# FFN second product of a two-layer decoder trunk: row tiles in written order in other PSUM banks, the next group's weight sums asked for between them

## The chip, the cores and the metric

One core of a Trainium2 chip runs the whole program. The metric is the device time of one execution in microseconds, the median of several runs. All times below are microseconds (us) unless marked ns. The engines are named as in the profile: PE (TensorE, matmuls), DVE (VectorE), ACT (ScalarE), POOL, and SP, whose queue starts nearly all transfers.

## The reference

Two layers of a decoder trunk for 512 positions of width 1024, in float32. Each layer is a mixer (attention, retention, short convolution, gates, output projection) and then the part that the change touches, a gated MLP with a causal depthwise convolution:

```python
h = rmsnorm(x, norm_ffn_g[l])
gu = jnp.einsum('bsd,df->bsf', h, w_ffn_in[l])
g_ff, u_ff = gu[..., :D_FF], gu[..., D_FF:]          # D_FF = 2816
g_ff = causal_dwconv(g_ff, ffn_conv_w[l], ffn_conv_b[l])
x = x + jnp.einsum('bsf,fd->bsd', jax.nn.silu(g_ff) * u_ff, w_ffn_out[l])
```

## The kernel before, in words

Everything is held transposed: channels on the 128 partitions, 512 positions in the free dimension. x is 8 tiles of 128x512. To keep float32 precision each operand is split into a high and a low part (`split`, `split_w`: ACT casts the high part, DVE subtracts for the low part), and `mm3` issues three matmuls for each product: high x high, high x low, low x high. So each weight tile goes: one transfer on SP's queue into a `raw` buffer (4 of them, shared by all weights), a cast on ACT, a subtraction on DVE, into `hi` and `lo` buffers (3 each for the wide ones).

The FFN (`ffn`) handles the 22 channel tiles f of width 128 in three groups, `GROUPS = (5, 9, 8)`. For each f of a group the first product and the convolution give one tile `act`; then the second product adds the group's contribution to x.

- Group 0 (f = 0 to 4) uses `plain(f)`: two full products `pg` and `pu` of 24 matmuls with 512 columns. In between, `halves(k)` prepares the operands `X` of the other form (tiles xn, xt, X).
- Groups 1 and 2 (f = 5 to 13 and 14 to 21) use `seven(f)`: seven half-width products of 12 matmuls with 256 columns each, made from sums of the weights. DVE forms the sums s31 and s24 from the transfers raw_f0 and raw_f1 (the second half of s31 needs both), ACT and DVE split them into h31/l31 and h24/l24. The products land in two PSUM tiles, `pa` and `pb`. `pa` is overwritten several times; of the fifth product `pa` is added into the tile u by DVE (line 865), and only after that the seventh product may overwrite `pa`. Then come the convolution (ACT line 309, DVE lines 310 and 311, tile c), a Silu, the product u times c (DVE line 874), and the split into `act`.
- `rows(grp, f0, act, d)` is the second product for one row tile d of x: 3 matmuls of 512 columns for each f of the group into the PSUM tile `p2` (15, 27 or 24 matmuls), then DVE adds it to x[d] (line 888). For a group of more than 8, its weights come in two pieces.

PSUM has two pools of four banks, `main` and `aux`. pa, pb, pg, pu and p2 all use `main`.

Which instruction comes when on each engine is not written by hand: a list scheduler with its own estimates of time orders them at build time; each engine then runs its queue strictly in that order. `tc.high_priority()` lifts instructions (weights, their splits and sums), and `tc.keep_in_program_order` ties an instruction to the written order on its engine: it isn't put ahead of what is written before it, though what is written later may still be put ahead of it.

Names in the rows: buffer numbers and the layer's digit are left out, so p210L is p2 of group 1, row 0 (p200L: group 0, row 0; p223L: group 2, row 3), pa13L is pa of f = 13, s3114L is s31 of f = 14, h315L is h31 of f = 5, act13L is act of f = 13. hi_faL, hi_fbL, hi_w2L are the split weights.

Of the kernel before, what the change touches and what calls it, by code (L numbers as in the profile page):

```python
# [24 lines left out]
KT = D // P  # L25
# [3 lines left out]
FT = DFF // P  # L29

GROUPS = (5, 9, 8)
HALF = S // 2
BUCKETS = 32
MAX_DIST = 128
# [19 lines left out]
def trunk(ctx, tc, xT, wr, wh, wt, wda, wret, wsc, wo, wf, w2, par, lamp, relb, onehot, mask, rope, gtab, out):  # L54
# [32 lines left out]
    def run(steps):  # L87
        for _ in steps:
            pass
# [29 lines left out]
    def main(name):  # L119
        return pm.tile([P, S], F32, tag="main", name=name)  # L120

    def aux(name):
        return pa.tile([P, S], F32, tag="aux", name=name)
# [30 lines left out]
    def weights(src, name):  # L154
        return split_w(load_w(src, name), name)

    def mm3(o, a, b, start, stop, more=False):

        T.matmul(o, a[0], b[0], start=start, stop=False, skip_group_check=more)  # L159
        T.matmul(o, a[0], b[1], start=False, stop=False, skip_group_check=more)  # L160
        T.matmul(o, a[1], b[0], start=False, stop=stop, skip_group_check=more)  # L161

    def split(src, hi, lo, g=None):

# [602 lines left out]
    def ffn(l, fp):  # L767
# [4 lines left out]
        L = f"L{l}"  # L772
# [54 lines left out]
            V.tensor_tensor(u, u, c, ALU.mult)  # L827
            return split2(u, pairN(f"act{f}{L}"))

        def seven(f):  # L830
            upper, lower = [load_w(wf[l, f, :, b * D : (b + 1) * D], f"f{b}{L}{f}") for b in range(2)]
            a21, a11, a22, a12 = upper[:, :S], upper[:, S:], lower[:, :S], lower[:, S:]
            with tc.high_priority():
                w11 = split_w(a11, f"fa{L}{f}")
                s31 = fp.tile([P, 2, S], F32, tag="sum", name=f"s31{f}{L}", bufs=2)
                V.tensor_tensor(s31[:, 0], a21, a11, ALU.add)
                V.tensor_tensor(s31[:, 1], a21, a22, ALU.add)
                h31, l31 = slotX(f"h31{f}{L}"), slotX(f"l31{f}{L}")
                split(s31, h31, l31)
                s24 = fp.tile([P, 2, S], F32, tag="sum", name=f"s24{f}{L}", bufs=2)  # L840
                V.tensor_tensor(s24[:, 0], s31[:, 1], a11, ALU.add)
                V.tensor_tensor(s24[:, 1], s24[:, 0], a12, ALU.add)
                h24, l24 = slotX(f"h24{f}{L}"), slotX(f"l24{f}{L}")
                split(s24, h24, l24)
                w2212 = split_w(lower, f"fb{L}{f}")
            w22, w12 = [tuple(t[:, b * S : (b + 1) * S] for t in w2212) for b in range(2)]

            def product(o, w, b, start, stop):
# [27 lines left out]

        def rows(grp, f0, act, d):

            ps = main(f"p2{grp}{d}{L}")
            width = len(act)  # L880
            edge = min(width, KT // 2) if width > KT else 0
            for a, b in ((0, edge), (edge, width)):
                if a < b:
                    w = weights(w2[l, d, :, (f0 + a) * P : (f0 + b) * P], f"w2{L}{grp}{d}{a}")
                    for n in range(a, b):
                        sl = slice((n - a) * P, (n - a + 1) * P)
                        mm3(ps, (w[0][:, sl], w[1][:, sl]), act[n], n == 0, n == width - 1)
            V.scalar_tensor_tensor(x[d], ps, -1.0 if grp else 1.0, x[d], ALU.mult, ALU.add)
            if l == DEPTH - 1 and grp == len(GROUPS) - 1:
                nc.sync.dma_start(out[:, d], x[d])  # L890

        f0 = 0
        todo = list(range(KT // 2))
        for grp, width in enumerate(GROUPS):
            act = []
            for f in range(f0, f0 + width):
                act.append(seven(f) if grp else plain(f))
                if f == 1:
                    late.close()
                if grp == 0 and f and todo:  # L900
                    halves(todo.pop(0))
            for d in range(KT):
                rows(grp, f0, act, d)
            f0 += width

    for l in range(DEPTH):
# [107 lines left out]
```

## Time and profile before

| | us |
|---|---|
| median of 3 runs | 1522.0 |
| lowest and highest run | 1521.76, 1523.62 |
| the profiled execution's own time | 1522.98 |
| its span, first to last instruction | 1521.2 |
| PE busy | 1512.6 (99%) |
| DVE busy | 1105.0 (73%) |
| ACT busy | 734.0 (48%) |
| transfers, mean | 97 GB/s |

The profile is of one execution. Its own time is 1.8 above its span. The granted TensorE clock is 1.00 over the whole span. Matmuls overlap in the records: a matmul of 512 columns is shown with 390 ns while the next starts 227 ns after it, so time that PE lost is read from the distance of the starts, not from the column of idle time alone.

### The profile page before, as it was taken

How to read it: one execution, taken by the hardware profiler on the slowest of the kernel's cores; microseconds unless marked ns; L12 is line 12 of the kernel's file. 1: busy time of each engine (PE TensorE's matmuls, PEld its weight loads, DVE VectorE, ACT ScalarE, POOL GpSimd, SP SyncE). 2: the span in 40 equal slices, each digit the busy share in tenths (PEclk: the TensorE clock that was granted, in tenths of full speed). 3: DMA queues.
4: the chain of work that ended last, by engine and by line, in shares of the span. 5: the costliest groups of instructions: out<-in, count | busy, mean ns of one | idle time of the engine just before them, and what ended most of it. 6: DMA issues, size and time to landing. Idle time of an engine off the chain costs nothing.

```text
span 1521.2 us, 22083 instructions
## 1 busy us (share of the span) xinstructions
PE 1512.6 (99%) x8510; PEld 1338.7 (88%) x8510; DVE 1105.0 (73%) x2074; ACT 734.0 (48%) x1304; POOL 13.0 (1%) x26
## 2 busy tenths in 40 slices
PE   9999999999999999999999999999999999999998
PEld 7899988888888999899789999888888889988996
DVE  8588787554688995796656887875545889947963
ACT  4555665333454564464425565643333546634641
POOL 1000000000000000000100000000000000000000
PEclk9999999999999999999999999999999999999999
DMA  6322222232323322522322222222322233324322
GB/s 212 115 73 81 86 84 90 76 104 83 106 74 107 118 92 72 169 84 84 131 77 94 74 91 87 83 84 83 106 88 86 79 113 112 97 84 139 111 59 81
DMA packets 51146, 147.24 MB, mean 97 GB/s; under 512 B 5624, under 2 KB 6023, under 8 KB 51041
## 3 DMA queue, kind: packets, MB, share of 16 engines
q1 hardware_dynamic: 50224, 143.38, 28.7%
q0 software_dynamic: 816, 2.46, 0.6%
q8 instruction: 67, 1.10, 0.3%
q14 instruction: 39, 0.31, 0.1%
HBM read 143.70 MB, written 2.11 MB: 96 GB/s over the span
## 4 chain that ended last, share of the span: by engine, by line
PE 97%; DVE 1%; DMA 1%; issue 0%; ACT 0%; SPq 0%; ACTq 0%; DVEq 0%
PE pnrvgL L161 1%; PE pnrvgL L159 1%; PE pnrvgL L160 1%; PE pnrqkL L160 1%; PE pnrqkL L161 1%; PE pnrqkL L159 1%; PE pnh2L L161 1%; PE pnh2L L159 1%; PE pnh3L L160 1%; PE pnh3L L161 1%; PE pnh1L L161 1%; PE pnh2L L160 1%; PE pnh3L L159 1%; PE pnh1L L160 1%; PE pnh1L L159 1%; PE pnh0L L160 1%
## 5 line engine op out<-in xcount | busy, mean ns | idle before, releaser
L150 ACT CAST hi_tL<-raw_tL 128x1024 fp32r<-128x1024 f32 x60 | 62.9, 1049 | 115.3 <-issue 14.7
L150 ACT CAST hi_w2L<-raw_w2L 128x640 fp32r<-128x640 f32 (+2 forms) x64 | 49.1, 782 | 94.0 <-PE p210L L160 11.2
L151 DVE TENSOR_TENSOR lo_tL<-raw_tL,hi_tL 128x1024 fp32r<-128x1024 f32 x60 | 73.4, 1223 | 15.9 <-ACT hi_tL L150 15.5
L151 DVE TENSOR_TENSOR lo_w2L<-raw_w2L,hi_w2L 128x640 fp32r<-128x640 f32 (+2 forms) x64 | 55.8, 888 | 29.5 <-ACT hi_w2L L150 29.5
L150 ACT CAST hi_fbL<-raw_f1L 128x1024 fp32r<-128x1024 f32 x34 | 35.7, 1051 | 32.3 <-PE pa5L L160 5.7
L150 ACT CAST hi_oL<-raw_oL 128x1024 fp32r<-128x1024 f32 x16 | 16.9, 1054 | 58.1 <-issue 18.7
L151 DVE TENSOR_TENSOR lo_fbL<-raw_f1L,hi_fbL 128x1024 fp32r<-128x1024 f32 x34 | 41.6, 1222 | 1.5 <-ACT hi_fbL L150 1.4
L150 ACT CAST hi_faL<-raw_f0L 128x512 fp32r<-128x512 f32 x34 | 21.1, 620 | 30.7 <-DMA raw_f0L<-in_wf 12.8
L151 DVE TENSOR_TENSOR lo_faL<-raw_f0L,hi_faL 128x512 fp32r<-128x512 f32 x34 | 23.4, 689 | 4.0 <-ACT hi_faL L150 3.9
L150 ACT CAST hi_nrvgL<-raw_nrvgL 128x1024 fp32r<-128x1024 f32 x8 | 8.4, 1051 | 29.7 <-PE pnrvgL L161 13.5
L150 ACT CAST hi_fuL<-raw_fuL 128x1024 fp32r<-128x1024 f32 x10 | 10.5, 1054 | 22.9 <-issue 17.1
L151 DVE TENSOR_TENSOR lo_oL<-raw_oL,hi_oL 128x1024 fp32r<-128x1024 f32 x16 | 19.6, 1224 | 2.8 <-ACT hi_oL L150 2.8
L151 DVE TENSOR_TENSOR lo_nrvgL<-raw_nrvgL,hi_nrvgL 128x1024 fp32r<-128x1024 f32 x8 | 9.8, 1226 | 12.4 <-ACT hi_nrvgL L150 12.4
L150 ACT CAST hi_fgL<-raw_fgL 128x1024 fp32r<-128x1024 f32 x10 | 10.5, 1050 | 14.8 <-issue 13.0
L151 DVE TENSOR_TENSOR lo_nh0L<-raw_nh0L,hi_nh0L 128x768 fp32r<-128x768 f32 x8 | 7.7, 958 | 13.1 <-ACT hi_nh0L L150 13.1
L150 ACT CAST hi_bdL<-raw_bdL 128x512 fp32r<-128x512 f32 x16 | 9.9, 618 | 12.6 <-issue 4.2
L150 ACT CAST hi_nrqkL<-raw_nrqkL 128x1024 fp32r<-128x1024 f32 (+1 forms) x9 | 8.4, 948 | 13.9 <-issue 13.9
L151 DVE TENSOR_TENSOR lo_fuL<-raw_fuL,hi_fuL 128x1024 fp32r<-128x1024 f32 x10 | 12.2, 1222 | 2.9 <-ACT hi_fuL L150 2.9
L150 ACT CAST hi_nh0L<-raw_nh0L 128x768 fp32r<-128x768 f32 x8 | 6.7, 838 | 15.2 <-PE pnh0L L161 7.8
L151 DVE TENSOR_TENSOR lo_nrqkL<-raw_nrqkL,hi_nrqkL 128x1024 fp32r<-128x1024 f32 (+1 forms) x9 | 9.9, 1109 | 5.2 <-ACT hi_nrqkL L150 5.2
L151 DVE TENSOR_TENSOR lo_fgL<-raw_fgL,hi_fgL 128x1024 fp32r<-128x1024 f32 x10 | 12.2, 1222 | 0.8 <-ACT hi_fgL L150 0.8
L150 ACT CAST hi_nh3L<-raw_nh3L 128x768 fp32r<-128x768 f32 x8 | 6.7, 838 | 11.5 <-PE ptg16L L160 5.3
(8471 smaller groups left out, 5969.6 us busy)
## 6 DMA issues: line engine op xcount, KB each, us to landing
raw_tL<-in_wt SPq DMA_DIRECT2D x60, 512.0 KB, 3.3
raw_f0L<-in_wf SPq DMA_DIRECT2D x34, 512.0 KB, 3.8
raw_f1L<-in_wf SPq DMA_DIRECT2D x34, 512.0 KB, 3.7
raw_w2L<-in_w SPq DMA_DIRECT2D x32, 320.0 KB, 2.9
raw_oL<-in_wo SPq DMA_DIRECT2D x16, 512.0 KB, 3.4
raw_w2L<-in_w SPq DMA_DIRECT2D x16, 512.0 KB, 3.5
raw_fgL<-in_wf SPq DMA_DIRECT2D x10, 512.0 KB, 4.0
raw_fuL<-in_wf SPq DMA_DIRECT2D x10, 512.0 KB, 4.0
```

Source lines behind the costliest of these rows:

```text
L150: A.copy(h, raw)
L151: V.tensor_tensor(w, raw, h.bitcast(F32), ALU.subtract)
L159: T.matmul(o, a[0], b[0], start=start, stop=False, skip_group_check=more)
L160: T.matmul(o, a[0], b[1], start=False, stop=False, skip_group_check=more)
L161: T.matmul(o, a[1], b[0], start=False, stop=stop, skip_group_check=more)
```

## The change

`mm3` gets an option that ties its matmuls to the written order, and `rows` uses it. `rows` takes its PSUM tile from `aux` instead of `main`. It becomes a generator that stops ahead of the last f of its group, and the loop first runs 2, 1 and 1 row tiles (`AHEAD`) of groups 0, 1 and 2 up to that point; then all row tiles are run to their ends one after the other. `seven` is cut in two: `sums(f)` (transfers, sums, splits of the sums) and the products; inside a group the sums of f + 1 are written ahead of the products of f, and the sums of the first two f of the next group are written behind row tiles 2 and 5 (`EARLY`) of this one. The split of the lower weights moves from the sums to the products.

```diff
+AHEAD = (2, 1, 1)
+EARLY = (2, 5)
@@
-    def mm3(o, a, b, start, stop, more=False):
-
-        T.matmul(o, a[0], b[0], start=start, stop=False, skip_group_check=more)
-        T.matmul(o, a[0], b[1], start=False, stop=False, skip_group_check=more)
-        T.matmul(o, a[1], b[0], start=False, stop=stop, skip_group_check=more)
+    def mm3(o, a, b, start, stop, more=False, queue=False):
+
+
+        for i, (p, q) in enumerate(((0, 0), (0, 1), (1, 0))):
+            t = T.matmul(o, a[p], b[q], start=start and i == 0, stop=stop and i == 2, skip_group_check=more)
+            if queue:
+                tc.keep_in_program_order(t)
@@
-        def seven(f):
+        def sums(f):
+
             upper, lower = [load_w(wf[l, f, :, b * D : (b + 1) * D], f"f{b}{L}{f}") for b in range(2)]
@@
                 split(s24, h24, l24)
-                w2212 = split_w(lower, f"fb{L}{f}")
+            return lower, w11, h31, l31, h24, l24
+
+        def seven(f, lower, w11, h31, l31, h24, l24):
+            w2212 = split_w(lower, f"fb{L}{f}")
@@
-            ps = main(f"p2{grp}{d}{L}")
+            ps = aux(f"p2{grp}{d}{L}")
@@
                     for n in range(a, b):
+                        if n == width - 1:
+                            yield
                         sl = slice((n - a) * P, (n - a + 1) * P)
-                        mm3(ps, (w[0][:, sl], w[1][:, sl]), act[n], n == 0, n == width - 1)
+                        mm3(ps, (w[0][:, sl], w[1][:, sl]), act[n], n == 0, n == width - 1, queue=True)
@@
+        made = {}
         for grp, width in enumerate(GROUPS):
             act = []
             for f in range(f0, f0 + width):
-                act.append(seven(f) if grp else plain(f))
+                if grp:
+                    for n in (f, f + 1):
+                        if n < f0 + width and n not in made:
+                            made[n] = sums(n)
+                    act.append(seven(f, *made[f]))
+                else:
+                    act.append(plain(f))
@@
+
+            begun = [rows(grp, f0, act, d) for d in range(KT)]
+            for d in range(AHEAD[grp]):
+                next(begun[d])
             for d in range(KT):
-                rows(grp, f0, act, d)
+                run(begun[d])
+                if d in EARLY and grp + 1 < len(GROUPS):
+                    n = f0 + width + EARLY.index(d)
+                    made[n] = sums(n)
```

The number of instructions is the same on every engine; only their order changes, and the lines are numbered some lines later. Three places of the new order follow; layer 1 has the same order at each of them.

The first is DVE at the end of group 0, from the first use of the last product (u4 = pu4 times the norm) to the low part of act4. X2 and X3 are operands that `halves` prepares, s315 is the weight sum of f = 5. Before:

```order
L167 TENSOR_TENSOR X2L_3927<-xt2L_4309,X2L_3927 128x1024
L826 TENSOR_TENSOR u4L_4388<-pu4L_4351,rBfL_4030 128x512
L796 SCALAR_TENSOR_TENSOR xn3L_4394<-x_85,par_110,rBfL_4030 128x512
L796 SCALAR_TENSOR_TENSOR xn7L_4396<-x_89,par_110,rBfL_4030 128x512
L151 TENSOR_TENSOR lo_w2L_4459<-raw_w2L_4456,hi_w2L_4458 128x640
L827 TENSOR_TENSOR u4L_4388<-u4L_4388,c4L_4359 128x512
L800 TENSOR_TENSOR xt3L_4398<-xn3L_4394 128x256
L167 TENSOR_TENSOR X3L_3928<-xn3L_4394,X3L_3928 128x256
L802 TENSOR_TENSOR xt3L_4398<-xn7L_4396,xn3L_4394 128x256
L167 TENSOR_TENSOR X3L_3928<-xn7L_4396,X3L_3928 128x512
L801 SCALAR_TENSOR_TENSOR xt3L_4398<-xt3L_4398,xn7L_4396 128x256
L167 TENSOR_TENSOR act4L_4391<-u4L_4388,act4L_4391 128x512
```

With the change, from u4 to the last row ahead of act4:

```order
L832 TENSOR_TENSOR u4L_4388<-pu4L_4351,rBfL_4030 128x512
L173 TENSOR_TENSOR X2L_3927<-xt2L_4309,X2L_3927 128x1024
L802 SCALAR_TENSOR_TENSOR xn3L_4394<-x_85,par_110,rBfL_4030 128x512
L802 SCALAR_TENSOR_TENSOR xn7L_4396<-x_89,par_110,rBfL_4030 128x512
L155 TENSOR_TENSOR lo_w2L_4459<-raw_w2L_4456,hi_w2L_4458 128x640
L833 TENSOR_TENSOR u4L_4388<-u4L_4388,c4L_4359 128x512
L806 TENSOR_TENSOR xt3L_4398<-xn3L_4394 128x256
L843 TENSOR_TENSOR s315L_4486<-raw_f0L_4478 128x512
L844 TENSOR_TENSOR s315L_4486<-raw_f0L_4478,raw_f1L_4480 128x512
L173 TENSOR_TENSOR X3L_3928<-xn3L_4394,X3L_3928 128x256
L808 TENSOR_TENSOR xt3L_4398<-xn7L_4396,xn3L_4394 128x256
L173 TENSOR_TENSOR X3L_3928<-xn7L_4396,X3L_3928 128x512
```

After these come, as before, the last small xt3 and then act4. Three instructions, the wide split X2 and the two halves of s315, now stand between u4 and act4. On PE, between the last matmul of pu4 and the first matmul that needs the low part of act4, there stand 25 matmuls of 512 columns (24 of row tiles 0 and 1, one of act4's high part) and 14 of 256 columns (pa5 and the start of pb5); before, there were 36 of row tiles 0, 1 and 2 and three of act4's high part.

The second place is PE at the end of group 1: the last matmuls of pa13's fifth product, the seventh product (its weights are hi_fb, lo_fb), and the first row tile. Before:

```order
L161 MATMUL pa13L_5643<-X3L_3928,l3113L_5629 128x256
L159 MATMUL p210L_5745<-act11L_5486,hi_w2L_5766 128x512
L160 MATMUL p210L_5745<-act11L_5486,hi_w2L_5766 128x512
L161 MATMUL p210L_5745<-act11L_5486,lo_w2L_5767 128x512
L159 MATMUL p210L_5745<-act12L_5614,hi_w2L_5766 128x512
L159 MATMUL p211L_5786<-act5L_4718,hi_w2L_5789 128x512
L160 MATMUL p211L_5786<-act5L_4718,hi_w2L_5789 128x512
```

16 more matmuls of p210 and p211 follow before the seventh product begins, 22 in all. With the change:

```order
L165 MATMUL pa13L_5643<-X3L_3928,h3113L_5522 128x256 x2
L165 MATMUL pa13L_5643<-X3L_3928,l3113L_5523 128x256
L165 MATMUL pa13L_5643<-X0L_3925,hi_fbL_5639 128x256 x2
L165 MATMUL pa13L_5643<-X0L_3925,lo_fbL_5640 128x256
L165 MATMUL pa13L_5643<-X1L_3926,hi_fbL_5639 128x256 x2
L165 MATMUL pa13L_5643<-X1L_3926,lo_fbL_5640 128x256
L165 MATMUL pa13L_5643<-X2L_3927,hi_fbL_5639 128x256 x2
L165 MATMUL pa13L_5643<-X2L_3927,lo_fbL_5640 128x256
L165 MATMUL pa13L_5643<-X3L_3928,hi_fbL_5639 128x256 x2
L165 MATMUL pa13L_5643<-X3L_3928,lo_fbL_5640 128x256
L165 MATMUL p210L_5745<-act5L_4740,hi_w2L_5748 128x512 x2
L165 MATMUL p210L_5745<-act5L_4740,lo_w2L_5749 128x512
```

The seventh product now follows the fifth at once, and all 27 matmuls of p210 stand behind it, then p211 and so on. pa21 at the end of group 2 is the same: 24 matmuls of pa21 in a row (before, 12 of pb21, 3 of p220 and 9 of p221 stood between the two products), then p220 to p227, each whole.

The third place is DVE at the same time: from pb13's addition to the low part of u13's product. s3114 and s2414 are the weight sums of f = 14. Before:

```order
L867 TENSOR_TENSOR pad_116<-pad_116,pb13L_5644 128x512
L865 TENSOR_TENSOR u13L_5645<-u13L_5645,pa13L_5643 128x256
L310 SCALAR_TENSOR_TENSOR c13L_5736<-pad_116,par_110,c13L_5736 128x512
L311 SCALAR_TENSOR_TENSOR c13L_5736<-pad_116,par_110,c13L_5736 128x512
L151 TENSOR_TENSOR lo_w2L_5872<-raw_w2L_5869,hi_w2L_5871 128x512
L151 TENSOR_TENSOR lo_w2L_5849<-raw_w2L_5846,hi_w2L_5848 128x640
L874 TENSOR_TENSOR u13L_5645<-u13L_5645,c13L_5736 128x512
L167 TENSOR_TENSOR act13L_5742<-u13L_5645,act13L_5742 128x512
```

With the change:

```order
L877 TENSOR_TENSOR pad_116<-pad_116,pb13L_5644 128x512
L844 TENSOR_TENSOR s3114L_5876<-raw_f0L_5868,raw_f1L_5870 128x512
L875 TENSOR_TENSOR u13L_5645<-u13L_5645,pa13L_5643 128x256
L848 TENSOR_TENSOR s2414L_5883<-s3114L_5876,raw_f0L_5868 128x512
L316 SCALAR_TENSOR_TENSOR c13L_5736<-pad_116,par_110,c13L_5736 128x512
L849 TENSOR_TENSOR s2414L_5883<-s2414L_5883,raw_f1L_5870 128x512
L173 TENSOR_TENSOR l3114L_5880<-s3114L_5876,h3114L_5879 128x1024
L317 SCALAR_TENSOR_TENSOR c13L_5736<-pad_116,par_110,c13L_5736 128x512
L155 TENSOR_TENSOR lo_w2L_5849<-raw_w2L_5846,hi_w2L_5848 128x640
L173 TENSOR_TENSOR l2414L_5887<-s2414L_5883,h2414L_5886 128x1024
L884 TENSOR_TENSOR u13L_5645<-u13L_5645,c13L_5736 128x512
L155 TENSOR_TENSOR lo_w2L_5831<-raw_w2L_5828,hi_w2L_5830 128x512
```

act13's low part is the next row. The second half of s3114, which reads the transfer raw_f1 of f = 14, stands ahead of the addition of pa13, and five instructions on the sums of f = 14 stand between pb13 and u13's product. On SP, raw_f0 and raw_f1 of f = 14 stand behind the weights of row tiles 0 to 2; with four raw buffers, raw_f1 takes the one of row tile 1's second piece of weights, which is free once DVE has split that piece (lo_w2L_5808, five rows above the first row shown, behind the first half of s3114 and both taps of c12). The cast ahead of that split takes a `hi` buffer that PE frees near the end of pa12's seventh product; from there to pa13's seventh product PE has the last matmul of pa12, 1 and 24 of pb13 and 24 of pa13, all of 256 columns.

## Rows read from the trace of the kernel before

**Rows 1.** The profile's first part: engine, busy us (share of the span) and instructions.

```profile
PE 1512.6 (99%) x8510; PEld 1338.7 (88%) x8510; DVE 1105.0 (73%) x2074; ACT 734.0 (48%) x1304; POOL 13.0 (1%) x26
```

**Rows 2.** Who waited for whom on PE: line of the waiting matmul, what it waited for, total us, times, longest us. The idle time is counted from the modelled end of the matmul before.

```profile
PE pa5L L159 <- ACT pad L858: 1.6, 2, 1.0
...
PE p224L L159 <- ACT hi_w2L L150: 0.4, 2, 0.2
```

**Rows 3.** PE in order of time, two steady stretches (start us, duration us, engine, line, operation, tiles, shape): 512 columns, then 256 columns.

```profile
469.16 0.39 PE L159 MATMUL p200L<-act0L,hi_w2L 128*128 128x512 f32 x1
469.38 0.39 PE L160 MATMUL p200L<-act0L,hi_w2L 128*128 128x512 f32 x1
...
500.82 0.28 PE L160 MATMUL pa6L<-X3L,hi_faL 128*128 128x256 f32 x1
500.94 0.28 PE L161 MATMUL pa6L<-X3L,lo_faL 128*128 128x256 f32 x1
```

**Rows 4.** PE and ACT in order of time around pa5's second product (h245), layer 0 and layer 1 (in brackets the idle time before, and what ended it).

```profile
501.34 0.36 ACT L858 COPY pad<-pa5L 128x256 f32<-128x256 f32 x1
...
501.76 0.39 PE L159 MATMUL pa5L<-X0L,h245L 128*128 128x256 f32 x1 [0.54 <-ACT pad L858]
...
501.98 0.28 PE L160 MATMUL pa5L<-X0L,h245L 128*128 128x256 f32 x1
...
1254.74 0.28 PE L161 MATMUL pa6L<-X3L,lo_faL 128*128 128x256 f32 x1
1256.05 0.39 PE L159 MATMUL pa5L<-X0L,h245L 128*128 128x256 f32 x1 [1.03 <-ACT pad L858]
1256.27 0.28 PE L160 MATMUL pa5L<-X0L,h245L 128*128 128x256 f32 x1
```

**Rows 5.** PE in order of time where row tiles 3 to 5 of group 2 begin, first and last row of layer 0 and of layer 1; then ACT at the same place of layer 0.

```profile
734.07 0.39 PE L161 MATMUL p222L<-act21L,lo_w2L 128*128 128x512 f32 x1
...
736.70 0.40 PE L160 MATMUL p225L<-act14L,hi_w2L 128*128 128x512 f32 x1
...
1488.35 0.39 PE L161 MATMUL p222L<-act21L,lo_w2L 128*128 128x512 f32 x1
...
1490.98 0.39 PE L160 MATMUL p225L<-act14L,hi_w2L 128*128 128x512 f32 x1
...
733.37 2.94 ACT L150 CAST hi_w2L<-raw_w2L 128x1024 fp32r<-128x1024 f32 x3 [4.75 <-PE p220L L160]
```

**Rows 6.** PE in order of time where row tiles 3 to 5 of group 0 begin, first and last row of layer 0 and of layer 1.

```profile
479.36 0.40 PE L159 MATMUL p203L<-act0L,hi_w2L 128*128 128x512 f32 x1
...
480.84 0.40 PE L160 MATMUL p205L<-act0L,hi_w2L 128*128 128x512 f32 x1
...
1233.15 0.39 PE L159 MATMUL p203L<-act0L,hi_w2L 128*128 128x512 f32 x1
...
1234.63 0.40 PE L160 MATMUL p205L<-act0L,hi_w2L 128*128 128x512 f32 x1
```

**Rows 7.** DVE in order of time, layer 0: u4 and the low part of act4 at the end of group 0; then pairs of rows that show what one instruction of a kind takes from start to start (a tap of the convolution, a wide split, half of a weight sum).

```profile
469.36 0.69 DVE L826 TENSOR_TENSOR u4L<-pu4L,rBfL 128x512 f32<-128x512 f32 x1 [0.73 <-PE pu4L L161]
...
474.56 0.69 DVE L167 TENSOR_TENSOR act4L<-u4L,act4L 128x512 fp32r<-128x512 f32 x1
...
456.67 0.75 DVE L311 SCALAR_TENSOR_TENSOR c3L<-pad,par,c3L 128x512 f32<-128x512 f32 x1
457.33 1.22 DVE L167 TENSOR_TENSOR X1L<-xt1L,X1L 128x1024 fp32r<-128x1024 f32 x1
...
498.24 1.23 DVE L151 TENSOR_TENSOR lo_fbL<-raw_f1L,hi_fbL 128x1024 fp32r<-128x1024 f32 x1
499.37 1.23 DVE L167 TENSOR_TENSOR l316L<-s316L,h316L 128x1024 fp32r<-128x1024 f32 x1
...
503.44 0.70 DVE L836 TENSOR_TENSOR s317L<-raw_f0L 128x512 f32<-128x512 f32 x1
504.04 0.70 DVE L837 TENSOR_TENSOR s317L<-raw_f0L,raw_f1L 128x512 f32<-128x512 f32 x1
```

**Rows 8.** The turn of pa's fifth product at f = 21, layer 0: its last matmul on PE, and the addition on DVE that waits for it.

```profile
719.24 0.28 PE L161 MATMUL pa21L<-X3L,l3121L 128*128 128x256 f32 x1
...
719.56 0.42 DVE L865 TENSOR_TENSOR u21L<-u21L,pa21L 128x256 f32<-128x256 f32 x1 [4.83 <-PE pa21L L161]
```

**Rows 9.** The profile's list of transfers: count, KB each, median us from issue to landing.

```profile
raw_f1L<-in_wf SPq DMA_DIRECT2D x34, 512.0 KB, 3.7
```

**Rows 10.** ACT and DVE in order of time at the end of group 1, layer 0: the cast of the second piece of a row tile's weights, which waits for pa12, and its split; pa13's addition with the row behind it; u13's product and the low part of act13.

```profile
585.47 0.73 ACT L150 CAST hi_w2L<-raw_w2L 128x640 fp32r<-128x640 f32 x1 [1.98 <-PE pa12L L160]
...
586.23 0.83 DVE L151 TENSOR_TENSOR lo_w2L<-raw_w2L,hi_w2L 128x640 fp32r<-128x640 f32 x1 [2.54 <-ACT hi_w2L L150]
...
591.11 0.42 DVE L865 TENSOR_TENSOR u13L<-u13L,pa13L 128x256 f32<-128x256 f32 x1 [0.75 <-PE pa13L L161]
591.45 0.74 DVE L310 SCALAR_TENSOR_TENSOR c13L<-pad,par,c13L 128x512 f32<-128x512 f32 x1
...
598.94 0.68 DVE L874 TENSOR_TENSOR u13L<-u13L,c13L 128x512 f32<-128x512 f32 x1
600.31 0.69 DVE L167 TENSOR_TENSOR act13L<-u13L,act13L 128x512 fp32r<-128x512 f32 x1 [0.69 <-ACT act13L L166]
```

**Rows 11.** The chain of waits around the first sums of group 1, layer 1: a transfer beside others (start us, us from issue to landing).

```profile
1235.82 5.73 DMA raw_f0L<-in_wf
```

## The prediction

> **What bounds the kernel now.** I read the share of busy time first. PE is busy for 1512.6 of the span of 1521.2 us, DVE for 73%, ACT for 48% [rows 1]. The kernel is bound by PE, and the change neither adds nor removes an instruction; so it can only give back time in which PE stands still, or add some. Next come the waits of PE [rows 2]: they name pa5, which waits for ACT, and the row tiles of group 2, which wait for casts of weights. As the ends of matmuls are modelled, I take the lost time from the starts. In a steady stretch a matmul of 512 columns starts 0.227 us after the one before (469.16 to 469.38) and one of 256 columns 0.12 after it (500.82 to 500.94) [rows 3]; what is longer is lost. Measured so, the FFN loses time at three places in each layer:
>
> - Row tiles 3 to 5 of group 2. From 734.07 to 736.70 there are six steps: 2.63 - 6 x 0.227 = 1.27, and in layer 1 from 1488.35 to 1490.98 the same [rows 5]. Tiles 0 to 2 wait for act21 together, end together, and free three weight buffers at once; the three casts of tiles 3 to 5 take 2.94 in a row, while PE has only two matmuls for each.
> - Row tiles 3 to 5 of group 0, the same in small: 1.48 - 5 x 0.227 = 0.35 in each layer [rows 6].
> - pa5's second product. In layer 0 its first matmuls are at 501.76 and 501.98, the last before them at 500.94 [rows 3, 4]: 1.04 - 2 x 0.12 = 0.80. In layer 1 it is 1.53 - 0.24 = 1.29. ACT's copy of pa5 is late there, behind casts of late weights.
>
> Together 2 x (1.27 + 0.35) + 0.80 + 1.29 = 5.3 us. That is all the change can win in the FFN. A measurement of this kernel can tell a change of 0.2%, 3.0 us, from none.
>
> **What the change removes.** With each row tile run whole, a tile's weights come free 12 to 27 matmuls apart, at least 2.7 us, and a wide cast takes about 1 (2.94 for three) [rows 5]: the two bursts go, -3.2 in all. The first sums of group 1 are asked for some row tiles earlier, so pa5's first product and its copy lie between the row tiles, and the wait of 0.80 and 1.29 goes, -2.1. Putting p2 in other banks gives nothing by itself: what pa5 waits for is a copy out of its own bank [rows 4], not a row tile's.
>
> **What it adds.** The filling matmuls that stood between dependent products are now tied behind them. I go through the FFN's dependent places, for one layer.
>
> (1) act4, end of group 0. On DVE the low part of act4 ends at 475.25, 5.89 after u4 starts [rows 7]. The new order puts a wide split (1.13, from 498.24 to 499.37) and two halves of a sum (0.60 each, 503.44 to 504.04) in between [rows 7]: 8.22. PE starts the row tiles 0.20 before u4 (469.16, 469.36) [rows 3, 7] and has 25 matmuls of 512 columns and 14 of 256 until it needs that part: 25 x 0.227 + 14 x 0.12 = 7.35, so it is there at 7.15. From the end of a releaser to PE's start take 0.06 (501.34 + 0.36 to 501.76) [rows 4]. Wait: 8.22 + 0.06 - 7.15 = 1.13. The first matmul after a wait also costs some 0.10 more (501.76 to 501.98 is 0.22, not 0.12) [rows 4]; this and the wait for h315 just before overlap, so I take **1.2**. Bounds: 0.7 if DVE gets one half of the sum done earlier, 1.5.
>
> (2) pa21, end of group 2. The seventh product now stands right behind the fifth, with DVE's addition between. The addition starts 0.32 after the last matmul's start (719.24, 719.56) and takes 0.42 [rows 8], then 0.06: 0.80 - 0.12 = 0.68, and 0.10 for the slow first matmul: **0.78**. Nothing covers it. Bounds: 0.6 to 0.9.
>
> (3) pa13, end of group 1: the same 0.78 at least, but DVE's queue now holds the second half of s3114 ahead of the addition, and that waits for the transfer raw_f1 of f = 14. Its buffer is freed by the split of row tile 1's second piece, that by a cast which starts when pa12's seventh product lets go of a buffer. Call the cast's start 0. PE's matmul that releases it began 0.32 earlier [rows 8], and with it and 50 more of 256 columns PE is ready for the seventh product at 51 x 0.12 - 0.32 = 5.80. The cast takes 0.73, the split 0.83 and can start at 0.76 [rows 10]; but the first half of s3114 and the two taps of c12 (0.60 + 2 x 0.66, 456.67 to 457.33) [rows 7] stand ahead of it, and no row tells how much of them is left. I take a third, 0.6: the split ends at 2.19, the transfer lands 3.7 later [rows 9] at 5.89, the half sum (0.60) and the addition (0.42) end near 6.95, PE starts at 7.03. Wait 1.23, with the slow start **1.3**. Bounds: 0.78 if the taps are done, 2.6 if none is.
>
> (4) act13, same place. From the addition's start DVE has, in its new order, 0.34 (591.11 to 591.45), two halves of s2414 (2 x 0.60), two taps (2 x 0.66), two wide splits (2 x 1.13) and a split of weights (0.74): 5.86; from u13's product to the end of act13's low part before were 2.06 (598.94 to 601.00) [rows 7, 10]: 7.92, with 0.06 7.98. PE starts the seventh product at 0.48, loses 0.10, has 12 x 0.12 and 25 x 0.227: 7.70. Wait 0.28, with a slow start **0.4**. Bounds: 0 to 0.8. For act21 no sums stand in the way; 2.06 and two taps are well under the 21 x 0.227 = 4.8 of row tile 0.
>
> Sum for a layer 1.2 + 0.78 + 1.3 + 0.4 = 3.7, for both 7.4. Against 5.3 that is +2.1; the transfers being moved earlier on SP's queue cost nothing else, as SP waits for buffers and not for issue, and 16 engines' transfers average 97 GB/s. The profiled execution's span becomes 1523.3 and its own time 1525.0; this execution was 1.0 above the median of 1522.0, so the median becomes **1524.0 us**. Own range by the bounds: 2 x (0.7 + 0.6 + 0.78 + 0) = 4.2 to 2 x (1.5 + 0.9 + 2.6 + 0.8) = 11.6, so 1520.9 to 1528.3, the upper bounds together being unlikely.
>
> A rule that speaks for the change: the Trainium skill, "Perfetto Trace Analysis", section Optimizing Tensor Performance, says that independent groups of matmuls should rotate through different PSUM banks, so that emptying one overlaps the next. By that rule alone, taking p2 out of pa's banks would shorten every handover. By the rows it does nothing here, since the waits are inside one bank (pa) or on weights; where it would lead is rival C.
>
> **Rivals.**
>
> A. It evens out. pa13's transfer is early, (3) falls to 0.78 and (4) to nothing, (1) to 0.9: 2 x 2.5 = 5.0 against 5.3, 1521.7 us. For it: DVE idles before some of these rows (2.54 before the split) [rows 10], so the taps may be done.
>
> B. Slower beyond 0.2%. The transfers of the next group's sums now run among those of the row tiles' weights, and DVE's queue holds instructions that wait for them ahead of what PE needs. Beside others a raw_f0 took 5.73 [rows 11], not 3.7. If raw_f1 of f = 14 takes that, (3) grows by 2.0, in two layers by 4.0: 1528.0 us. It decides as soon as the transfer lands 0.5 later than I take it (2 x 0.5 more makes +3.1). Against it: at that point SP has just waited for a buffer, so little should be under way.
>
> C. Faster. The waits of 5.3 go and none comes, because ACT and DVE are free enough to feed row tiles one by one and the handovers overlap: 1516.7 us. Against it: (2) has no cover at all in the new order, on PE or elsewhere.
>
> That the change doesn't do what it says is ruled out by the new order; but "begun ahead" does nothing at groups 1 and 2, where row tile 0 stands behind all products.
>
> **How the numbers follow.** My forecast 0.55, of which a tenth lies above +3.0; A 0.17, B 0.22, C 0.06. Faster by over 0.2%: 0.06; within: 0.50 + 0.17 = 0.67; slower: 0.22 + 0.05 = 0.27. The range for 8 in 10 leaves out C and the worst of B: from 1521.0, the forecast's lower bound, to 1527.2.
>
> **What would show it right or wrong.** Right: the steps at row tiles 3 to 5 are steady, pa5's second product doesn't wait, and PE loses time instead ahead of p200 (on act4), between the two last products of pa13 and of pa21 (on DVE's line 875), and near the end of p210 (on act13). Wrong: pa21 without a gap; a gap at pa13 over 2 us, released behind a transfer; or new gaps at the first products of a group (pa5, pa14), which I cost at nothing because their weights are asked for several row tiles ahead.

## The result, and the profile after

The changed kernel takes 1525.1 us (median) against 1522.1 for the kernel before beside it: ratio 1.0018, 95% interval 1.0010 to 1.0026, or +3.05 us (1.5 to 4.0). Run again unaltered beside others (`after_again`) it was 1525.3 against 1523.0, ratio 1.0014 (1.0006 to 1.0023), +2.3. The forecast was 1524.0, +2.0: a little slower, at the edge of 0.2%.

The busy shares hardly move against [rows 1]; the waits of PE [rows 2] have other names. First the profile's first part, then who waited for whom on PE (total us, times, longest us), both of the changed kernel:

```profile
PE 1512.4 (99%) x8510; PEld 1340.1 (88%) x8510; DVE 1106.9 (73%) x2074; ACT 734.5 (48%) x1304; POOL 13.0 (1%) x26
```

```profile
PE pa13L L165 <- DVE u13L L875: 1.8, 2, 1.2
PE p200L L165 <- DVE act4L L173: 1.2, 2, 0.6
...
PE pa21L L165 <- DVE u21L L875: 1.0, 2, 0.5
```

pa5 and the row tiles of group 2 are gone from the list, and three of the prediction's four places stand in it; the fourth, act13, is too short for the list. What each costs is read from the starts. "Lost time" below is that: the distance from start to start, less 0.227 or 0.12.

**The bursts are gone.** PE in the changed kernel, group 2 of layer 0, from the end of row tile 2 to the start of row tile 6:

```profile
735.52 0.39 PE L165 MATMUL p222L<-act21L,lo_w2L 128*128 128x512 f32 x1
735.74 0.62 PE L165 MATMUL p223L<-act14L,hi_w2L 128*128 128x512 f32 x2
...
752.06 0.62 PE L165 MATMUL p226L<-act14L,hi_w2L 128*128 128x512 f32 x2
```

Those are 73 steps in 16.54 us, 0.227 each; where [rows 5] lost 1.27, nothing is lost.

**act4.** PE and DVE in the changed kernel at the end of group 0, layer 0 (in brackets the idle time before, and what ended it):

```profile
475.12 0.40 PE L165 MATMUL p200L<-act4L,hi_w2L 128*128 128x512 f32 x1
475.35 0.28 PE L165 MATMUL pa5L<-X3L,hi_faL 128*128 128x256 f32 x1
475.47 0.28 PE L165 MATMUL pa5L<-X3L,lo_faL 128*128 128x256 f32 x1
475.83 0.50 PE L165 MATMUL pb5L<-X0L,h315L 128*128 128x256 f32 x2
476.96 0.50 PE L165 MATMUL p200L<-act4L,hi_w2L 128*128 128x512 f32 x1 [0.62 <-DVE act4L L173]
```

```profile
468.66 0.69 DVE L832 TENSOR_TENSOR u4L<-pu4L,rBfL 128x512 f32<-128x512 f32 x1 [1.26 <-PE pu4L L165]
469.27 1.22 DVE L173 TENSOR_TENSOR X2L<-xt2L,X2L 128x1024 fp32r<-128x1024 f32 x1
...
473.40 0.69 DVE L843 TENSOR_TENSOR s315L<-raw_f0L 128x512 f32<-128x512 f32 x1
474.00 0.69 DVE L844 TENSOR_TENSOR s315L<-raw_f0L,raw_f1L 128x512 f32<-128x512 f32 x1
...
476.22 0.69 DVE L173 TENSOR_TENSOR act4L<-u4L,act4L 128x512 fp32r<-128x512 f32 x1
```

From u4 to act4's low part DVE takes 476.22 + 0.69 - 468.66 = 8.25 (forecast 8.22; 5.89 before). With the short wait for h315, PE loses 0.35 at pb5 and 0.89 at p200: 1.24 in each layer.

**pa5.** The last matmul of pa5's first product is the row at 475.47 above. The first of its second product (h245) comes at:

```profile
496.48 0.28 PE L165 MATMUL pa5L<-X0L,h245L 128*128 128x256 f32 x1
```

92 matmuls (19.6 us) lie between the two products, against 24 (2.9) in the kernel before; ACT's copy has all that time, and nothing is lost.

**pa13.** DVE and PE in the changed kernel at the end of group 1, layer 1:

```profile
1334.75 0.69 DVE L843 TENSOR_TENSOR s3114L<-raw_f0L 128x512 f32<-128x512 f32 x1 [0.96 <-DMA raw_f0L<-in_wf]
1335.36 0.75 DVE L316 SCALAR_TENSOR_TENSOR c12L<-pad,par,c12L 128x512 f32<-128x512 f32 x1
1336.14 0.75 DVE L317 SCALAR_TENSOR_TENSOR c12L<-pad,par,c12L 128x512 f32<-128x512 f32 x1
1336.81 0.82 DVE L155 TENSOR_TENSOR lo_w2L<-raw_w2L,hi_w2L 128x640 fp32r<-128x640 f32 x1
...
1341.24 0.69 DVE L844 TENSOR_TENSOR s3114L<-raw_f0L,raw_f1L 128x512 f32<-128x512 f32 x1 [0.86 <-DMA raw_f1L<-in_wf]
1341.85 0.41 DVE L875 TENSOR_TENSOR u13L<-u13L,pa13L 128x256 f32<-128x256 f32 x1
```

```profile
1340.82 0.28 PE L165 MATMUL pa13L<-X3L,l3113L 128*128 128x256 f32 x1
1342.32 0.50 PE L165 MATMUL pa13L<-X0L,hi_fbL 128*128 128x256 f32 x2 [1.22 <-DVE u13L L875]
```

PE is released by the addition (line 875), but that waits behind the second half of s3114, that for raw_f1, whose buffer the split at 1336.81 frees, and that stands behind a sum that waits for raw_f0. So two transfers of f = 14 are in series here. Their issues on SP's queue, raw_f0 of layer 0 first, then both of layer 1:

```profile
575.30 0.33 SPq L141 DMA_DIRECT2D raw_f0L<-in_wf  x1
...
1329.91 0.71 SPq L141 DMA_DIRECT2D raw_f0L<-in_wf  x1
1337.66 0.33 SPq L141 DMA_DIRECT2D raw_f1L<-in_wf  x1
```

raw_f1 is issued 0.03 after the split ends (1336.81 + 0.82). PE loses 1.49 with the slow first matmul; in layer 0, 0.82.

**act13.** PE near the end of p210, and the low part of act13 on DVE, layer 0:

```profile
594.03 1.02 PE L165 MATMUL p210L<-act13L,hi_w2L 128*128 128x512 f32 x2
594.89 0.40 PE L165 MATMUL p210L<-act13L,lo_w2L 128*128 128x512 f32 x1
```

```profile
593.80 0.69 DVE L173 TENSOR_TENSOR act13L<-u13L,act13L 128x512 fp32r<-128x512 f32 x1
```

The second of the two merged matmuls needs the low part, which ends at 594.49; two steps take 0.86 instead of 0.45, so 0.40 is lost.

**pa21.** PE and DVE in the changed kernel, layer 0: the turn of [rows 8] (last matmul of the fifth product, DVE's addition, first matmul of the seventh) with nothing between, the bare turn below:

```profile
717.08 0.28 PE L165 MATMUL pa21L<-X3L,l3121L 128*128 128x256 f32 x1
717.87 0.50 PE L165 MATMUL pa21L<-X0L,hi_fbL 128*128 128x256 f32 x2 [0.51 <-DVE u21L L875]
```

```profile
717.39 0.42 DVE L875 TENSOR_TENSOR u21L<-u21L,pa21L 128x256 f32<-128x256 f32 x1 [0.75 <-PE pa21L L165]
```

0.79 - 0.12 and 0.10 behind it: 0.78.

### The profile page after: what moved, and what is told of

It is laid out like the page before. It is cut to its first block, busy times and chain, and to the rows that moved or that the text cites. A ratio compares the mean times of both kernels' runs of the same rounds, so it can differ in the third digit from the quotient of the medians.

```text
span 1522.4 us, 22092 instructions
## 1 busy us (share of the span) xinstructions
PE 1512.4 (99%) x8510; PEld 1340.1 (88%) x8510; DVE 1106.9 (73%) x2074; ACT 734.5 (48%) x1304; POOL 13.0 (1%) x26
## 4 chain that ended last, share of the span: by engine, by line
PE 96%; DVE 2%; DMA 1%; issue 0%; ACT 0%; SPq 0%; ACTq 0%; DVEq 0%
PE pnrvgL L165 3%; PE pnrqkL L165 2%; PE pnh2L L165 2%; PE pnh3L L165 2%; PE pnh1L L165 2%; PE pnh0L L165 2%; PE pb20L L165 1%; PE pb10L L165 1%; PE p214L L165 1%; PE p213L L165 1%; PE p217L L165 1%; PE p216L L165 1%; PE p211L L165 1%; PE p215L L165 1%; PE p212L L165 1%; PE pa21L L165 1%
## 5 line engine op out<-in xcount | busy, mean ns | idle before, releaser
L155 DVE TENSOR_TENSOR lo_oL<-raw_oL,hi_oL 128x1024 fp32r<-128x1024 f32 x16 | 19.6, 1224 | 2.8 <-ACT hi_oL L154 2.8
```

What stands on the lines that cost most here:

```text
L155: V.tensor_tensor(w, raw, h.bitcast(F32), ALU.subtract)
```

## The experiments

The theory (W): what the FFN's gaps sum to is the whole cost. Rivals: the tie or the banks cost something that no gap shows; the early transfers do it by themselves. All runs in one table. "FFN lost" sums the steps of both layers from the first product to the last row tile; the next column is that less the 5.36 of the kernel before, which the theory says the medians should show. Each median stands against the kernel before in its own comparison.

| kernel | FFN lost, us | less 5.36 | median less before | ratio, 95% interval |
|---|---|---|---|---|
| the change | 3.28 + 3.95 = 7.23 | +1.9 | +3.05 | 1.0010 to 1.0026 |
| after_again | 3.56 + 4.34 = 7.90 | +2.5 | +2.3 | 1.0006 to 1.0023 |
| early_36 | 1.65 + 1.65 = 3.30 | -2.1 | -1.8 | 0.9979 to 0.9997 |
| untied | 1.48 + 2.94 = 4.42 | -0.9 | -0.2 | 0.9988 to 1.0006 |
| tie_only | 6.57 + 6.37 = 12.94 | +7.6 | +7.2 | 1.0033 to 1.0061 |
| banks_only | 1.85 + 3.35 = 5.20 | -0.2 | -0.3 | 0.9988 to 1.0005 |
| group0_36 | 2.08 + 3.35 = 5.43 | +0.1 | +0.2 | 0.9990 to 1.0008 |
| no_early | 1.43 + 1.30 = 2.73 | -2.6 | -2.2 | 0.9977 to 0.9995 |
| t222_36 | 0.12 + 0.12 = 0.24 | -5.1 | -4.6 | 0.9958 to 0.9981 |
| t222_none | 1.31 + 0.54 = 1.85 | -3.5 | -2.9 | 0.9974 to 0.9991 |
| tied_seven | 4.46 + 8.37 = 12.83 | +7.5 | +7.2 | 1.0035 to 1.0060 |
| none_ahead | 6.38 + 6.39 = 12.77 | +7.4 | +7.9 | 1.0038 to 1.0065 |

The lost time is that of one execution of each kernel, the medians are of 5 to 13 runs. In eleven kernels the two columns agree within 1.2, over a span of 12 us; to that accuracy the gaps are the cost.

**early_36: the early sums one row tile later.**

```diff
-EARLY = (2, 5)
+EARLY = (3, 6)
```

> The sums of the next group are written behind row tiles 3 and 6 instead of 2 and 5; everything else is the change. Theory (W): the time of the changed kernel is its four kinds of waits, per layer 1.24 ahead of act4's low part, 0.82 to 1.49 at pa13, 0.40 at act13, 0.78 at pa21, against 5.3 of waits in the kernel before. Here the wide split X2 stands ahead of u4 again, so act4 comes in time (the two halves of s315 add 1.2 to the 5.89 of before: 7.09, and PE arrives at 7.35), and no sum of f = 14 stands ahead of pa13's addition or act13. What is left is the bare turn of 0.78 at pa13 and at pa21: 2 x 1.56 = 3.1 against 5.3, so -2.2 against the kernel before (1519.9) and 4 below the changed one. Rival T (the tie or the banks cost PE time that no single gap shows; the medians are 3.05 apart, my gaps account for 1.85): the unexplained 1.2 stays, about 1521. Rival L (later requests make the first products of the groups late): new gaps of 0.8 to 1.3 at pa5 or pa14, 1522 to 1523.

1521.3 against 1523.0: -1.8, where W had -2.2. Of the FFN only the two bare turns are left in the list (who waited for whom):

```profile
PE pa21L L165 <- DVE u21L L875: 1.0, 2, 0.5
PE pa13L L165 <- DVE u13L L875: 1.0, 2, 0.5
```

So 7.23 - 3.30 = 3.9 of the change's lost time comes from where the early sums are asked for.

**group0_36: only group 1's sums later.**

```diff
-EARLY = (2, 5)
+EARLY = {0: (3, 6), 1: (2, 5), 2: ()}
```

> The change, but the sums of group 1 (f = 5 and 6) are written behind row tiles 3 and 6 of group 0; those of group 2 stay behind row tiles 2 and 5 of group 1. DVE's order at the end of group 1 is that of the change, word for word; at the end of group 0 the wide split X2 stands ahead of u4. Theory W, with the waits of group 1 put down to f = 14's sums in DVE's queue and to the transfer behind them: the 1.24 ahead of act4 falls to 0.1, pa13 keeps 0.8 to 1.5 and act13 its 0.40, pa21 its 0.78: 2 x 1.1 = 2.3 under the changed kernel, 0.4 under the kernel before. Rival (the waits of group 1 come from the row tiles' order or from what went before, not from these sums): pa13 falls to 0.78 and act13 to nothing, as they did when both groups were moved.

It takes 0.2 more than the kernel before and 2.2 less than the change beside it. The 1.24 falls to 0.11, act13 keeps 0.40, pa21 0.78. pa13 loses 0.78 in layer 0 and 2.00 in layer 1 under the same order, so W holds and the rival does not. DVE in `group0_36`, layer 0, then layer 1:

```profile
580.55 0.69 DVE L843 TENSOR_TENSOR s3114L<-raw_f0L 128x512 f32<-128x512 f32 x1
...
587.27 0.69 DVE L844 TENSOR_TENSOR s3114L<-raw_f0L,raw_f1L 128x512 f32<-128x512 f32 x1
587.92 0.42 DVE L875 TENSOR_TENSOR u13L<-u13L,pa13L 128x256 f32<-128x256 f32 x1
...
1335.14 0.69 DVE L843 TENSOR_TENSOR s3114L<-raw_f0L 128x512 f32<-128x512 f32 x1 [1.13 <-DMA raw_f0L<-in_wf]
...
1341.98 0.69 DVE L844 TENSOR_TENSOR s3114L<-raw_f0L,raw_f1L 128x512 f32<-128x512 f32 x1 [1.33 <-DMA raw_f1L<-in_wf]
```

In layer 0 the first sum does not wait and the second hardly (0.10), and the turn is bare; in layer 1 both wait. From issue to landing raw_f0 of f = 14 took 3.83 in layer 0 and 4.98 in layer 1 here; 4.18 and 4.82, 4.09 and 5.01 in the two executions of the change, with 0.82, 1.49, 1.08 and 1.86 lost. raw_f1 took 3.5 to 3.9 in all six. As the two are in series, both count: that layer 1 loses more comes from raw_f0, while in layer 0 the two executions of the change differ (0.82, 1.08) by raw_f1, which took 3.53 and 3.86 there. A fifth raw buffer, which would take the two transfers out of series, was not tried.

**no_early: the change without early sums.**

```diff
-EARLY = (2, 5)
+EARLY = ()
```

> The change without early sums: those of each group's first f are asked for behind the row tiles, as before the change; banks, tie and row tiles begun ahead stay. Theory W: no wide split and no sum stands ahead of act4, and PE does 27 matmuls of 512 columns (6.1) before it needs act4's low part (0.20 + 5.89 + 0.06): a wait of 0.1 to 0.5; pa13 has 8 matmuls of pb13 between its last products (0.96 against the turn of 0.8) and no gap; act13 none; pa21 0.78; pa5's first product comes only with row tile 7, and its second product waits for the copy again, by 0.8 to 1.9. Together 1.7 to 3.2 a layer, about the 5.4 of the kernel before or 1 above: 0 to +1. So the early sums would give 2.1 to 3.8 at pa5 and cost 2 x (1.1 + 0.7 + 0.4), a net loss as they stand. Rival: pa5's wait doesn't come back (its cure is the row tiles' order): 2 to 3 under the kernel before.

The rival held: 2.2 under the kernel before, and 4.5 under the change beside it. act4 loses 0.59 a layer, a little more than W's 0.5; pa13 and act13 lose nothing, pa21 0.78. pa5's wait does not come back (0.10 in layer 0, none in layer 1). What it is shows on ACT of the kernel before, layer 1, and of `no_early`, layer 0:

```profile
1254.16 1.05 ACT L150 CAST hi_fbL<-raw_f1L 128x1024 fp32r<-128x1024 f32 x1 [2.31 <-DMA raw_f1L<-in_wf]
...
1255.63 0.36 ACT L858 COPY pad<-pa5L 128x256 f32<-128x256 f32 x1
```

```profile
501.31 1.05 ACT L154 CAST hi_fbL<-raw_f1L 128x1024 fp32r<-128x1024 f32 x1 [4.86 <-DMA raw_f1L<-in_wf]
...
502.78 0.36 ACT L868 COPY pad<-pa5L 128x256 f32<-128x256 f32 x1
```

In both, pa5's copy stands in ACT's queue behind a cast that waits for a later f's transfer. In `no_early` the scheduler puts 35 matmuls (4.2 us) between pa5's first two products instead of 24, which just cover it. `t222_none` has the same order there and lost 0.75 at pa5 in layer 0: the cover is thin. So the early sums are not needed to avoid the wait, but with their 92 matmuls they take it off the edge. The number of matmuls is not all of it: `tie_only` has the same 24 as the kernel before and no wait at pa5, in either layer; PE comes there some 4.6 later by what it lost before.

**tie_only, banks_only, untied: the parts by themselves.** The first is the kernel before with the tie, the second with the banks, the third the change without the tie:

```diff
-mm3(ps, (w[0][:, sl], w[1][:, sl]), act[n], n == 0, n == width - 1)
+mm3(ps, (w[0][:, sl], w[1][:, sl]), act[n], n == 0, n == width - 1, queue=True)
```

```diff
-            ps = main(f"p2{grp}{d}{L}")
+            ps = aux(f"p2{grp}{d}{L}")
```

```diff
-mm3(ps, (w[0][:, sl], w[1][:, sl]), act[n], n == 0, n == width - 1, queue=True)
+mm3(ps, (w[0][:, sl], w[1][:, sl]), act[n], n == 0, n == width - 1)
```

> The kernel before with nothing but the row tiles' matmuls tied to the written order: banks, requests and sums as before. Theory W: the row tiles run whole but with no cover: at the end of group 0 PE has 14 matmuls of 512 columns (3.2 us) until it needs act4, which comes 5.89 + 0.2 later, so some 3.1 is lost there, in place of the 1.2; pa13 and pa21 each lose the bare turn of 0.78; pa5's first products come behind all row tiles and wait for a copy some 0.6. About 5.2 a layer, 10.4 in both, against 5.3: +5 against the kernel before (1527). Rival T' (the written order is what removes the bursts and costs little): +0 to +2. Rival B (the changed kernel's cost is the early transfers and sums, which are missing here): no slower than the kernel before.

> The kernel before with p2 in the other pool of PSUM banks and nothing else. Theory W: the waits are inside pa's bank or on weights, so the banks move nothing by themselves: within 1 us of the kernel before, with some of the wait at pa5 (0.8 and 1.3) gone or moved as the scheduler fills differently. Rival (rotation through other banks shortens each handover, as the rule on banks would have it): at least -2, with the waits at pa5 and at the row tiles gone.

> The change without the tie of the row tiles' matmuls to the written order; banks, row tiles begun ahead and early sums stay. The scheduler may again put matmuls of row tiles between the dependent products. Theory W: the gaps at pa13 and pa21 (0.82 to 1.49 and 0.78) go, as row tiles stand between fifth and seventh product there; in exchange several row tiles end together, and the bursts come back (group 0 about 1.0 to 1.6, group 2 some 0.2) with a wait at pa5 of up to 1.7: some 3.5 a layer in all, 7 for both, about the changed kernel, +1.5 to +2.5 against the kernel before. Rival T (the tie itself costs): the time falls by more than the gaps say, to the kernel before or under it, though its bursts are back.

banks_only: nothing in sum, as W had it; pa5 lost 0.18 in layer 0 and 1.68 in layer 1, against 0.80 and 1.29. By the Trainium skill's rule on rotating banks ("Perfetto Trace Analysis", Optimizing Tensor Performance) the handovers should have become shorter; the ratio shows no gain. untied: W's number missed, -0.2 and not +1.5 to +2.5. Bursts are back, with waits of 1.1 at p203, pa13 and pa21 are covered, pa5 lost 1.45 in one layer and nothing in the other: 4.4 in all, less than W's 7, which had put up to 1.7 on pa5 and up to 1.6 on group 0 in each layer. The time is rival T's, but not its reason: it doesn't fall by more than the gaps say (-0.9). tie_only: no burst is left at the row tiles, so the tie alone removes them; the direction is W's, but +7.2 and not +5. PE around act4 in `tie_only`, layer 0, and stretches of the same (PE busy, weight loads, DVE, ACT, POOL, granted clock, share of transfers, GB/s):

```profile
474.25 0.49 PE L160 MATMUL p200L<-act4L,hi_w2L 128*128 128x512 f32 x1 [1.37 <-ACT act4L L167]
476.14 0.50 PE L160 MATMUL p200L<-act4L,hi_w2L 128*128 128x512 f32 x1 [1.40 <-DVE act4L L168]
...
478.59 0.63 PE L160 MATMUL p201L<-act1L,lo_w2L 128*128 128x512 f32 x1
479.01 1.05 PE L160 MATMUL p201L<-act2L,hi_w2L 128*128 128x512 f32 x2
```

```profile
474.00:476.00 2.00, 0.49 (x1) 0.19 (x1) 2.00 (x5) 0.19 (x1) 0.00 (x0) 1.00 0.52 160
476.00:478.00 2.00, 1.85 (x6) 1.51 (x7) 1.50 (x4) 1.54 (x2) 0.00 (x0) 0.76 0.00 0
478.00:480.00 2.00, 2.00 (x6) 1.52 (x6) 1.50 (x2) 0.13 (x1) 0.00 (x0) 0.50 0.00 0
```

Two waits of 1.53 and 1.67 stand close together, and behind them the granted clock is 0.50 for some 3 us: 512 columns take 0.42 from start to start (478.59 to 479.01). That adds 1.6 a layer to the 3.2.

**none_ahead: the banks and the tie alone.**

```diff
-AHEAD = (2, 1, 1)
-EARLY = (2, 5)
+AHEAD = (0, 0, 0)
+EARLY = ()
```

> The change without early sums and with no row tile begun ahead: p2 in the other banks and tied to the written order, nothing else. PE's order is that of the kernel before with the tie alone, but for the banks. Theory W: the same loss as there, 6.5 a layer: 3.2 in two waits ahead of act4, then some 1.7 in which matmuls of 512 columns start 0.43 instead of 0.227 apart (granted clock 0.50), 0.78 at pa13 and at pa21: +7 to +8 on the kernel before. Against the version without early sums (two row tiles begun ahead) that prices the begun row tiles at 9 to 10 us. Rival (the fall of the clock there was a thing of that one execution): +4.

+7.9, with the clock at 0.50 again in both layers: it is no accident of one execution, and the rival falls. Against `no_early` the row tiles begun ahead are worth 10.0 us of lost time: the waits ahead of act4, the clock behind them, and the turn at pa13.

**tied_seven: a product between pa's last two, one row tile begun.**

```diff
-            product(b[:, :HALF], w12, 1, False, True)
+            product(b[:, :HALF], w12, 1, False, True, last)
...
-            product(a, w22, 6, False, True)
+            product(a, w22, 6, False, True, last)
```

> The change, with the sixth and seventh products of each group's last f tied to the written order (pb's 12 matmuls between pa's last two products) and nothing else: the early sums stay behind row tiles 2 and 5, one row tile is begun ahead in groups 1 and 2. Theory W: the turn at pa13 and pa21 is covered, -0.8 to -1.6 and -0.78 a layer; but pb13's addition, and with it taps, Silu and act13, now come 1.44 later against PE, behind the same sums of f = 14 in DVE's queue. From pb13's addition to act13's low part the changed kernel takes 9.4 (585.08 to 594.5); PE has 12 x 0.12 + 24 x 0.227 = 6.9 for it: 2.5 to 3.4 lost at p210. act4's 1.24 stays. About 4.7 a layer, 9.4 in all against 7.2 in the changed kernel: +2 on it, +4 on the kernel before. So the covering product pays only with more row tiles begun ahead. Rival (one row tile is cover enough, act13 is on time): 2 x 2 = 4 under the changed kernel.

Slower, as W had it, but +7.2 and not +4: 2.9 lost at p210 in layer 0, but 3.9 in layer 1, where raw_f0 of f = 14 took 5.21 (3.71 in layer 0), and there the clock fell once more. The wait of PE, and stretches of layer 1 (columns as above) with the wait in the first:

```profile
PE p210L L165 <- ACT act13L L172: 5.3, 2, 3.1
```

```profile
1350.00:1354.00 4.00, 0.88 (x2) 0.29 (x1) 2.60 (x4) 1.25 (x2) 0.00 (x0) 0.84 0.37 108
1354.00:1359.00 5.00, 5.00 (x13) 3.91 (x13) 1.42 (x2) 0.72 (x1) 0.00 (x0) 0.50 0.19 55
```

**t222_36 and t222_none: the version that beats both.** `tied_seven` with `AHEAD = (2, 2, 2)`, and `EARLY = (3, 6)` or `()`.

> A version meant to beat both: the early sums behind row tiles 3 and 6; two row tiles begun ahead in each group; and for each group's last f the sixth and seventh products tied to the written order, so that pb's 12 matmuls (1.44) stand between pa's fifth and seventh product, where the turn of 0.8 lies. Theory W: the last waits, 0.78 at pa13 and at pa21, are covered; begun ahead, row tiles 0 and 1 (42 to 48 matmuls of 512 columns, 9.5 us and more) cover act13 and act21. Left: 0.1 to 0.3 a layer. 2 x 1.56 = 3.1 under the version with only the early sums moved, about 5 under the kernel before: 1518. Rival (act13 or act21 late: with the sixth product before the seventh, the convolution starts no later, but u's last product ends the same and the two row tiles don't suffice): a new wait at p210 or p220 of 1 to 3, and no gain over the version with the sums moved.

> The version with the tied sixth and seventh products and two row tiles begun ahead in each group, here without any early sums. Theory W as it now stands (the row tiles' order cured pa5, the early sums give nothing and cost where they stand ahead of what PE waits for): left is only the wait of 0.6 ahead of act4 that was there without early sums, 1.2 in all: 4 under the kernel before, within 1 of the version with early sums behind row tiles 3 and 6. Rival (early sums are what keeps pa5 and pa14 from waiting, and their absence was covered by chance before): a wait at pa5 of 0.8 to 1.9 a layer comes back, 1.5 to 4 slower than that version.

`t222_36` takes 1518.4 against 1523.0 of the kernel before, ratio 0.9969 (0.9958 to 0.9981), and 6.9 less than the change beside it. No place of the FFN is left in its list of waits; the two that stand there lie in the mixer and at the program's start:

```profile
PE pnrqkL L165 <- ACT hi_nrqkL L154: 1.4, 2, 0.9
PE ps_warm L196 <- POOL ones L190: 1.1, 1, 1.1
```

`t222_none` takes 1520.2: in it 0.6 a layer is back at act4 and 0.75 at pa5 in one layer. So here the early sums are worth 1.8 us between the medians of two comparisons, 1.6 in lost time. Without `tied_seven`'s order and the further row tiles begun they gain nothing: `early_36` 1521.3, `no_early` 1520.8.

`t222_36` differs from `tied_seven` in two things, the row tiles begun ahead and the place of the early sums, and no run separates them. In `t222_36` act13's low part ends at 594.65; row tile 0 starts at 587.69, so with that tile alone PE would have needed it 25 x 0.227 = 5.7 later, at 593.4. By this estimate the second row tile covers 1.3, and the rest of `tied_seven`'s 2.9 to 3.9 would be the sums' place.

## Why the prediction was right, and where not

| lost, us | forecast a layer | first execution, layer 0, 1 | second |
|---|---|---|---|
| (1) act4 | 1.2 | 1.24, 1.24 | 1.24, 1.24 |
| (2) pa21 | 0.78 | 0.78, 0.78 | 0.78, 0.78 |
| (3) pa13 | 1.3 | 0.82, 1.49 | 1.08, 1.86 |
| (4) act13 | 0.4 | 0.40, 0.40 | 0.41, 0.39 |
| both layers | 7.4 | 7.2 | 7.8 |

- What the change removes: right. Bursts and pa5's waits are gone, 5.3, the bursts by the tie alone (`tie_only`). pa5's first product lies between the row tiles, as said, with 92 matmuls of cover. But the early sums are not what it takes: without them (`no_early`) the 2.1 go as well, with 35 matmuls between pa5's products, and in `tie_only` with 24.
- (1), (2) and (4) hold to 0.04, with their mechanisms. (1) and (4) were worked out as a race of two queues: what stands on DVE from a known start, against what PE has to do until it needs it. (2) is a bare turn, priced from the same turn before.
- (3) is right in its mean, 1.31 over the four, but by luck, and with it the sum of 7.4. I put the size down to "a third" of the first half sum and the taps being left ahead of the split, 0.6. Split after cast was late by 0.28 in layer 0 of the first execution and by 0.92 in layer 1, 0.60 in the mean. What sets it is when raw_f0 of f = 14 lands, a transfer that the working left out; raw_f1's own 3.5 to 3.9 against the 3.7 taken adds the rest. The working's own terms also add up to 6.91 and 6.97, not 6.95 and 7.03, so to 1.17 and not 1.23.
- Rival B had the mechanism at the wrong transfer: raw_f1 took 3.5 to 3.9, about as taken, raw_f0 up to 5.0. It is why layer 1 loses more.
- Rival A falls with (1) and (4), though layer 0's pa13 came close to its 0.78. Rival C's 1516.7 falls; that its condition, no handover without cover, can be met with the same instructions is shown by `t222_36`.
- No new gap at the first products of the groups, as said. That "begun ahead" does nothing at groups 1 and 2 of the change was read from the order and not run; with the tied products of `t222_36` it covers some 1.3 at p210, by the estimate above.
- The profiled execution's span grew by 1.2, the FFN by 1.9: in stretches that the change doesn't touch, this execution lost 0.7 less than that of before. The medians' +3.05 and +2.3 lie around the FFN's 1.9 and 2.5; what remains is within their intervals.

## What to carry to other kernels

Where a kernel is bound by one engine, tying its order removes the filling work along with the disorder: list each dependent turn that the fill covered, and price it with the rows of the same turn before. An early request helps only if the instructions that wait for it do not come to stand, in an in-order queue, ahead of what the bound engine is about to need: the change's early sums cost 4.5 us against none (`no_early`), and asked for one row tile later about nothing; only with cover at every other turn did they gain 1.8. Begin independent work ahead of the last dependent step, and put an independent product between two that share a bank.

## What had not been expected of the hardware

A wait can be paid for twice. Behind two waits of 1.53 and 1.67 close together (`tie_only`, `none_ahead`, both layers) and in one of 3.28 with 0.50 behind it (`tied_seven`, layer 1) the granted clock fell from 1.00 to 0.50, that is from 2.4 to 1.2 GHz, and matmuls of 512 columns started 0.43 apart for 3 to 5 us; that cost another 1.6 to 2.5. Behind 2.33 and 0.50 (`tied_seven`, layer 0), and behind all waits of the change, it stayed at 1.00. That waits bring the lower clock back is also what the Trainium skill says ("TensorE: Matmul & The Clock Gate", HAM oscillation — how this bites in real kernels), there of a loop that waits for its transfers. These rows agree, with waits for ACT and DVE.

The same transfer of 512 KB at the same place of the two layers differed repeatably: raw_f0 of f = 14 took 3.7 to 4.2 in layer 0 and 4.8 to 5.2 in layer 1, in four executions each (two of the change, `group0_36`, `tied_seven`). Part of it lies in the issue: that instruction of SP's took 0.33 in layer 0 each time, and 0.71, 1.33, 1.37 and 0.99 in layer 1. In layer 1 a packet of 16 KB that the profile lists as `instruction` (queue q8) is under way just then: it starts 0.4 to 0.6 ahead of the issue and takes 0.9 to 1.4, and in layer 0 none is under way. From the transfers of the changed kernel between 1329 and 1335 us:

```profile
q8 instruction: 1, 0.02, 0.9%
```

That the packet is the cause is not shown. In layer 1 of `untied` such a packet also ran at the issue, but no weights of a row tile were still in flight there, and raw_f0 took 3.88, as in layer 0.
